# Building the first rows of a decoder trunk another way: where the modulation sums, the norm and the rows are made

## The chip, the cores and the metric

The kernel runs on one core of one Trainium2 chip. The metric is the device time of one execution in microseconds (us). A core has five engines that work beside each other, each through its own list of instructions in the order in which they stand: TensorE (PE, with its weight loads PEld), VectorE (DVE), ScalarE (ACT), GpSimd (POOL) and SyncE (SP), which here issues every DMA transfer. An engine that waits for another holds up all that stands behind in its own list.

## The reference

Two layers run over 256 tokens of width 2048: a retention mixer and then a gated short convolution, each followed by a SwiGLU feed-forward network. Ahead of every sub-layer the tokens are normalised and modulated by a conditioning vector `c`:

```python
def rms_norm(x, gain=None):
    xf = x.astype(jnp.float32)
    y = xf * lax.rsqrt(jnp.mean(xf * xf, axis=-1, keepdims=True) + EPS)
    if gain is not None:
        y = y * gain.astype(jnp.float32)
    return y

c_act = jax.nn.silu(c)
for i in range(DEPTH):                                            # DEPTH = 2
    mod = (c_act @ w_mod[i] + b_mod[i])[:, None, :]
    sh1, sc1, g1, sh2, sc2, g2 = jnp.split(mod, 6, axis=-1)       # each 2048 wide
    h = (rms_norm(x, norm1_g[i]) * (1.0 + sc1) + sh1).astype(x.dtype)
    # m = i % 4: 0 is retention, 1 is the short convolution
    x = (x + g1 * y).astype(x.dtype)                              # y is the mixer's output for h
    h = (rms_norm(x, norm2_g[i]) * (1.0 + sc2) + sh2).astype(x.dtype)
    x = (x + g2 * swiglu(h, ffn_w_in[i], ffn_w_out[i])).astype(x.dtype)
return rms_norm(x, final_g).astype(x.dtype)
```

The change touches the first `h` alone, which the retention mixer multiplies by its input weights (queries, keys, values and gates).

## The kernel before, in words

All activations lie with channels on the 128 partitions and the 256 tokens along them, so `x` and `h` are 16 rows of 128 channels each (KT = 16). "Row" always means such a block of 128 channels below.

Every float32 product is made of three products of parts kept in the type `fp32r`: high times high, high times low, low times high. So a weight block from memory is cut into a high part (`hi`, a CAST on ACT, L295) and a low part (`lo`, a subtraction on DVE, L296). The weights lie in memory in the order of their use, in pieces of 128 x 2048 (1 MiB each, one transfer). `prepare()` cuts half a piece, 128 x 1024, at a time; half a piece serves eight blocks of 128 x 128, which is 24 products on PE. Four `hi` and four `lo` buffers are used in turn, and three for the pieces as they come from memory. A row `h[k]` is cut into high and low in the same way.

A modulation value is a sum over 2048 products. One transfer brings 128 rows of `w_mod` (1 MiB), one DVE instruction over 128 x 2048 multiplies them by `cb`, the activated `c` on all partitions, and sums (L238), and one or two small POOL instructions add bias and gain (L243, L245, L248). Each row of the first `h` needs two of these: its scale (SC1) and its shift (SH1).

The first layer begins in two stages, and they are where the change is:

- **First stage** (`RET_FIRST`, lines 588 to 594). 16 column blocks (the first two heads' queries, keys and gates) are multiplied by the first `FIRST_KS = 11` rows, as soon as each row is made. Each row brings 48 products, one piece of weights (two halves) and two modulation sums: three transfers of 1 MiB. The order on DVE and ACT is as the code is written there (`tc.manual_schedule`).
- **Second stage** (lines 595 to 603). Three more heads' columns are multiplied by the same 11 rows, two column blocks at a time, in 12 groups. The sine and cosine tables (`angles`) and the five rows that are left are made beside it. Here a scheduler puts DVE's and ACT's instructions into an order; PE's and the transfers' order is as written. `held()` copies each finished group from PSUM with ACT (L569).

After that come the heads themselves (which add the products with the rows that were left out), the output projection, and the rest of the trunk. The order of PE's instructions is as written everywhere. Modulation sums of later sub-layers are spread over the whole run by a plan of PE's progress (`paced`).

The start is: `c` comes as one row, is spread to all partitions by products with ones (L199) and activated out of PSUM (L200); squares of the 16 rows of `x` on ACT (L387), added up on DVE (L388); sums over partitions on PE (L396), root by POOL's power (L407), spread on PE (L414), copied by ACT (L577). Then for each row k, in `row(k)` and `scale`:

- `scaled` (L424, DVE): u = x times scale column times root,
- `shifted` (L431, ACT): high part of u + shift, and (L432, DVE) its low part,
- the sum for SC1 of row k + 1 between these two, and the sum for SH1 of row k + 1 after half of row k's products.

Of the kernel before, what the change touches and what calls it, by code (L numbers as in the profile page):

```python
# [33 lines left out]
FIRST_KS = 11  # L34
EARLY_HEADS = 5
START_RAWS = 3
# [19 lines left out]
class Group:  # L56
    """Output columns of a matrix that are worked out together, in the order of their rows."""
# [60 lines left out]
def in_use_order():  # L118
    """Each group of the weights, with its matrix and the matrix's index, in the order of use."""
# [23 lines left out]
def laid_out(arrays):  # L143
    """The weights in the order of their use, as blocks of 128 rows and CHUNK columns."""
    total = sum(len(g.cols) * g.width * len(g.ks) for _, _, g in in_use_order())
    out = np.empty((total // CHUNK, P, CHUNK), np.float32)
    at = 0
    for key, i, g in in_use_order():
        for k in g.ks:
            for c in g.cols:  # L150
                o = at % CHUNK
                out[at // CHUNK, :, o : o + g.width] = arrays[key][i, k * P : (k + 1) * P, c : c + g.width]
                at += g.width
    assert at == total and total % CHUNK == 0
    return out
# [16 lines left out]
def trunk(ctx: ExitStack, tc: tile.TileContext, x_in, c_in, pos_in, w_mod, cols_in, tab_in, w_all, out):  # L172
# [8 lines left out]
    def name(s):  # L181
        serial[0] += 1
        return f"{s}_{serial[0]}"
# [10 lines left out]
    with tc.tile_pool(name="crow", bufs=1) as cp:  # L194
        row = cp.tile([1, D], F32, tag="row", name="row")
        nc.sync.dma_start(row, c_in)
        for i in range(0, D, 2 * S):
            pt = ps.tile([P, 2, S], F32, tag="bank", name=name("bank")).rearrange("p a b -> p (a b)")
            nc.tensor.matmul(pt, ones[0:1, :], row[:, i : i + 2 * S], start=True, stop=True)  # L199
            nc.scalar.activation(cb[:, i : i + 2 * S], pt, AF.Silu)  # L200
    x = []
    for i in range(0, KT, 4):
        t = const.tile([P, 4, S], F32, tag=f"x{i}", name=f"x{i}")
        nc.sync.dma_start(t, x_in[:, i : i + 4, :])
        x += [t[:, j, :] for j in range(4)]
    n_cols = cols_in.shape[1]
    cols = const.tile([P, n_cols], F32, tag="cols", name="cols")
    nc.sync.dma_start(cols, cols_in)
# [13 lines left out]
    nc.sync.dma_start(tab, tab_in[:, : 1 + P])  # L222
# [9 lines left out]
    def modulation(layer, which, j, pool=wpool, bufs=RAW_BUFS):  # L232
        t = layer * 6 * KT + which * KT + j
        raw = pool.tile([P, CHUNK], F32, tag="raw", name=name("raw"), bufs=bufs)
        nc.sync.dma_start(raw, w_mod[t])
        total = tmp("msum", (P, 1), bufs=4)
# [23 lines left out]
    def paced(n):  # L260
        """Counts n more products of 128 x 128 weights, and works out the modulations due by now."""
# [18 lines left out]
    ready, taken_cols, raws = [], [0], []  # L280

    def prepare():
# [5 lines left out]
        if i == 0:  # L288
            raw = wpool.tile([P, CHUNK], F32, tag="raw", name=name("raw"), bufs=RAW_BUFS)
            nc.sync.dma_start(raw, w_all[n * HALF // CHUNK])  # L290
            raws[:] = [raw]
# [9 lines left out]
    def take(group, k, col):  # L301
        """The next weights' high and low parts."""
# [18 lines left out]
    def ticked(n):  # L321
        """Between products, the next step of what runs beside them."""
# [5 lines left out]
    def product(g, act, base=0, before=None, banks=None, last=True):  # L328
        """Banks [columns, (high product, the rest), tokens], one for each of the group's columns."""
# [18 lines left out]
    def packed(g, act, base=0, before=None, between=None, banks=None):  # L348
        """Banks [columns, two of the group's columns, tokens]."""
# [25 lines left out]
    def split(dst, src, at=slice(0, S)):  # L375
        """dst [128, (high, low), tokens] of src."""
# [14 lines left out]
    def norm_sums(accs):  # L391
        """The sums over partitions, a token to a partition."""
# [9 lines left out]
    def norm_roots(pt, n):  # L402
        """1 / sqrt(mean + eps)."""
# [6 lines left out]
    def norm_spread(r):  # L410
        """The roots on all partitions, in PSUM."""
# [32 lines left out]
    def scaled_only(layer, norm, j):  # L444
        """h[j] without the norm and the shift."""
# [54 lines left out]
    def output(groups, act, which, last, after=None):  # L500
        """x += gate * product; if last, tiles whose sums are those of the new x's squares."""
# [24 lines left out]
    with ExitStack() as inner:  # L526
# [45 lines left out]
        with tc.tile_pool(name="start", bufs=1) as sp:  # L572
            acc = None
            for j in range(KT):
                acc = squares(acc, x[j])
            rb = tmp("rb", pool=sp, bufs=1)
            nc.scalar.copy(rb, rstd([acc], D))  # L577

            def scale(which, k):
                if k < KT:  # L580
                    modulation(0, which, k, sp, START_RAWS)

            def row(k):
                u = scaled(k, rb, 0, 0)
                scale(SC1, k + 1)
                shifted(h[k], u, k, 0, 0)

            with tc.manual_schedule(engines={mybir.EngineType.DVE, mybir.EngineType.Activation}):
                scale(SC1, 0)
                scale(SH1, 0)  # L590
                banks = [bank() for _ in range(8)]
                pts = packed(RET_FIRST, h, before=row, between=lambda k: scale(SH1, k + 1), banks=banks)
# [77 lines left out]
        def mixed(head, both, v, sg):  # L670
            """The rest of a head, in steps."""
# [32 lines left out]
        def pair(head, i):  # L704
            """Two columns' sums [columns, two, tokens]."""
# [143 lines left out]
```

## Time and profile before

| What | Value |
|---|---|
| Time, median of 3 runs | 2667.12 us (2664.53 to 2668.72) |
| Span of the profiled execution | 2660.6 us (first to last instruction) |
| PE busy | 2621.9 us, 99% of the span |
| DVE busy | 2017.8 us, 76% |
| ACT busy | 1248.4 us, 47% |
| POOL busy | 214.0 us, 8% |
| Transfers | 687.69 MB, mean 258 GB/s |
| Granted TensorE clock, mean | 0.998 |

The page gives the span and no other time of its execution; the span lies 6.5 us under the median of the timed runs. How to read it: busy times are sums of instructions' durations on an engine, and a PE product of 256 columns is shown with 0.28 us though a new one starts every 0.12 us, since products overlap in the array. So 99% says that PE almost always has something in flight. The first 40th of the span (66 us) is the exception: the row of busy tenths for PE begins with a 6.

### The profile page before, as it was taken

Reading aid. Unit: us, or ns where it says so; the run is one execution under the profiler, and the core shown is the slowest. Engines: PE = TensorE matmul, PEld = TensorE weight load, DVE = VectorE, ACT = ScalarE, POOL = GpSimd, SP = SyncE. Lnnn points to the kernel's source line nnn. Section 1 sums busy time; section 2 is a strip of 40 time slices with the busy share of each in tenths; the row PEclk is TensorE's granted clock in tenths of the full one; section 3 lists DMA queues with packets and bytes.
Section 4 is the critical chain, followed back from the end, with each engine's and each line's share of the span. In section 5 each row is a group of like instructions: output and inputs, shape, how many; then the busy total and the mean of one; then the engine's idle time right before and its main releaser. Section 6 shows DMA issues by size and latency. Waiting matters only on the chain.

```text
span 2660.6 us, 40134 instructions
## 1 busy us (share of the span) xinstructions
PE 2621.9 (99%) x16044; PEld 2335.6 (88%) x16044; DVE 2017.8 (76%) x2655; ACT 1248.4 (47%) x1782; POOL 214.0 (8%) x278
## 2 busy tenths in 40 slices
PE   6999999999999999999999999999999999999998
PEld 5898988999989888888888898888998888888887
DVE  8968988887698877777777889878887665555554
ACT  3444543444456444334444454444554443444443
POOL 4310000011000010100000001100000000000000
PEclk9999999999999999999999999999999999999999
DMA  9976667777677877777777768776777765555553
GB/s 374 400 265 242 251 217 296 267 270 263 250 267 261 312 281 267 298 271 284 285 268 282 268 219 321 287 282 256 268 269 256 264 220 190 185 185 189 189 190 127
DMA packets 96957, 687.69 MB, mean 258 GB/s; under 512 B 10753, under 2 KB 12545, under 8 KB 13825
## 3 DMA queue, kind: packets, MB, share of 16 engines
q1 hardware_dynamic: 96770, 685.13, 69.3%
q8 instruction: 125, 2.05, 0.3%
q14 instruction: 62, 0.51, 0.1%
HBM read 682.99 MB, written 2.10 MB: 257 GB/s over the span
## 4 chain that ended last, share of the span: by engine, by line
PE 76%; issue 19%; DVE 3%; DMA 0%; POOL 0%; ACT 0%; DVEq 0%; ACTq 0%; POOLq 0%
PE bank L338 35%; PE bank L341 18%; PE bank L363 4%; PE bank L361 4%; PE bank L362 4%; PE bank L634 2%; PE bank L635 2%; PE bank L636 2%; PE bank L477 1%; PE bank L476 1%; PE bank L478 1%; DVE raw L238 1%; DVE lo L296 1%; PE bank L680 0%; DMA raw<-w_mod 0%
## 5 line engine op out<-in xcount | busy, mean ns | idle before, releaser
L296 DVE TENSOR_TENSOR lo<-raw,hi 128x1024 fp32r<-128x1024 f32 x912 | 1113.5, 1223 | 561.1 <-ACT hi L295 559.2
L295 ACT CAST hi<-raw 128x1024 fp32r<-128x1024 f32 x912 | 953.9, 1050 | 1087.3 <-PE bank L338 638.5
L338 PE MATMUL bank<-h,hi 128*128 128x512 f32 x3296 | 1155.2, 395 | 0.0
L341 PE MATMUL bank<-h,lo 128*128 128x256 f32 x3296 | 925.5, 281 | 0.0
L338 PEld LDWEIGHTS bank<-h,hi 128*128 128x128 f32 x3296 | 622.7, 189 | 144.9
L338 PE MATMUL bank<-mid,hi 128*128 128x512 f32 x2100 | 731.1, 395 | 0.1
L341 PEld LDWEIGHTS bank<-h,lo 128*128 128x128 f32 x3296 | 623.3, 189 | 0.0
L341 PE MATMUL bank<-mid,lo 128*128 128x256 f32 x2100 | 583.8, 278 | 0.0
L338 PEld LDWEIGHTS bank<-mid,hi 128*128 128x128 f32 x2100 | 394.1, 188 | 92.2 <-DVE mid L378 0.4
L238 DVE SCALAR_TENSOR_TENSOR raw<-raw,cb 128x2048 f32<-128x2048 f32 x192 | 438.5, 2284 | 5.0 <-DMA raw<-w_mod 4.8
L341 PEld LDWEIGHTS bank<-mid,lo 128*128 128x128 f32 x2100 | 395.0, 188 | 0.0
L363 PE MATMUL bank<-h,lo 128*128 128x256 f32 x1024 | 292.4, 286 | 10.0 <-DVE lo L296 10.0
L361 PE MATMUL bank<-h,hi 128*128 128x256 f32 x1024 | 290.6, 284 | 2.8 <-ACT hi L295 2.8
L362 PE MATMUL bank<-h,hi 128*128 128x256 f32 x1024 | 290.3, 284 | 0.6 <-DVE h L432 0.5
L363 PEld LDWEIGHTS bank<-h,lo 128*128 128x128 f32 x1024 | 193.8, 189 | 14.4 <-DVE lo L296 14.4
L361 PEld LDWEIGHTS bank<-h,hi 128*128 128x128 f32 x1024 | 195.7, 191 | 3.5 <-ACT hi L295 3.3
L362 PEld LDWEIGHTS bank<-h,hi 128*128 128x128 f32 x1024 | 193.9, 189 | 2.3 <-DVE h L432 2.3
L243 POOL TENSOR_SCALAR mcol<-msum,cols 128x1 f32<-128x1 f32 x64 | 63.6, 994 | 549.6 <-DVE raw L238 549.6
L634 PE MATMUL bank<-hi,h 128*128 128x512 f32 x256 | 101.4, 396 | 0.0
L635 PE MATMUL bank<-lo,h 128*128 128x512 f32 x256 | 101.0, 395 | 0.0
L636 PE MATMUL bank<-hi,h 128*128 128x512 f32 x256 | 101.0, 394 | 0.0
L370 ACT COPY low<-bank 128x256 f32<-128x256 f32 x254 | 90.7, 364 | 11.7 <-PE bank L341 9.0
(122 smaller groups left out, 1811.6 us busy)
## 6 DMA issues: line engine op xcount, KB each, us to landing
raw<-w_all SPq DMA_DIRECT2D x456, 1024.0 KB, 4.9
raw<-w_mod SPq DMA_DIRECT2D x192, 1024.0 KB, 5.0
x<-x_in SPq DMA_DIRECT2D x4, 512.0 KB, 5.7
out<-out SPq DMA_DIRECT2D x5, 256.0 KB, 2.9
decay<-tab_in SPq DMA_DIRECT2D x8, 128.0 KB, 3.0
out<-out SPq DMA_DIRECT2D x3, 128.0 KB, 2.3
out<-out SPq DMA_DIRECT2D x1, 384.0 KB, 2.7
cols<-cols_in SPq DMA_DIRECT2D x1, 160.0 KB, 7.2
```

The costliest lines, as they stand in the source:

```text
L238: nc.vector.scalar_tensor_tensor(raw, raw, 1.0, cb, op0=ALU.mult, op1=ALU.mult, accum_out=total)
L295: nc.scalar.copy(hi, raw)
L296: nc.vector.tensor_tensor(lo, raw, hi.bitcast(F32), op=ALU.subtract)
L338: nc.tensor.matmul(pt, hi, h, start=fresh and k == g.ks[0], stop=False, skip_group_check=True)
L341: nc.tensor.matmul(pt[:, 1, :], lo, h[:, 0, :], start=False, stop=last and k == g.ks[-1], skip_group_check=True)
L361: nc.tensor.matmul(pt, hi, h[:, 0, :], start=first, stop=False, skip_group_check=True)
L362: nc.tensor.matmul(pt, hi, h[:, 1, :], start=False, stop=False, skip_group_check=True)
L363: nc.tensor.matmul(pt, lo, h[:, 0, :], start=False, stop=last, skip_group_check=True)
L370: nc.scalar.copy(low[:, at], pt[:, 1, at])
L634: nc.tensor.matmul(o, ht[:, 0, :], hi, start=k == 0, stop=False)
L635: nc.tensor.matmul(o, ht[:, 0, :], lo, start=False, stop=False)
L636: nc.tensor.matmul(o, ht[:, 1, :], hi, start=False, stop=k == KT - 1)
```

## The change

- **c**: one transfer now writes `c` to all 128 partitions (`c_in.to_broadcast([P, D])`, 128 rows of 8 KiB), and one ACT instruction over 128 x 2048 activates it in place. The products with ones are gone.
- **Norm**: ACT squares `x` two rows at a time (8 instructions of 128 x 512), and PE sums all of them into one place, four products of one column for each; DVE's 15 additions are gone.
- **Normalised rows**: `norm_two` multiplies two rows of `x` by the root at once on DVE (128 x 512).
- **Columns**: for the first 16 rows, ACT makes scale and shift columns (`column`, 128 x 1) from the sums; POOL makes none of them any more. `gain_1` is prepared once.
- **Rows**: ACT makes each row twice from the normalised one with scale and shift, in full float32 and as the high part; DVE subtracts (128 x 256, two tensors).
- **Order**: both sums of row k + 1 stand together, after half of row k's products; then `norm_two` in every second row; then the second half's `lo`. Transfers are issued two rows ahead, with `START_RAWS = 4` buffers for `w_mod` instead of 3, and weights' pieces are fetched apart from being cut.
- **Span**: `FIRST_KS = 10`. So the first stage has 480 products instead of 528 and the second 720 instead of 792; six rows instead of five are made beside the second stage, and the 48 products of row 10 in the first stage go to the heads.
- In the second stage, the sums of `both_reduced` no longer carry the low priority `MOD_PRIO`.

The same change, cut to its core (removed comments and docstrings are left out):

```diff
-FIRST_KS = 11
+FIRST_KS = 10
-START_RAWS = 3
+START_RAWS = 4
...
-            acc = None
-            for j in range(KT):
-                acc = squares(acc, x[j])
-            rb = tmp("rb", pool=sp, bufs=1)
-            nc.scalar.copy(rb, rstd([acc], D))
-
-            def scale(which, k):
-                if k < KT:
-                    modulation(0, which, k, sp, START_RAWS)
-
-            def row(k):
-                u = scaled(k, rb, 0, 0)
-                scale(SC1, k + 1)
-                shifted(h[k], u, k, 0, 0)
+            def reduced(which, k):
+                if k < KT:
+                    raw = raws_of.pop((which, k))
+                    total = totals[which, k] = tmp("msum", (P, 1), bufs=4)
+                    nc.vector.scalar_tensor_tensor(raw, raw, 1.0, cb, op0=ALU.mult, op1=ALU.mult, accum_out=total)
+
+            def column(which, k):
...
+                nc.scalar.activation(dst, totals.pop((which, k)), AF.Identity, bias=bias, scale=scale)
+                return dst
...
+            def row(k, between=None):
+
+                a, b = column(SC1, k), column(SH1, k)
+                t = normed_x[k // 2][:, k % 2, :]
+                full = tmp("u", bufs=3)
+                nc.scalar.activation(full, t, AF.Identity, bias=b, scale=a)
+                nc.scalar.activation(h[k][:, 0, :], t, AF.Identity, bias=b, scale=a)
+                if between:
+                    between()
+                nc.vector.tensor_tensor(
+                    h[k][:, 1, :], full, h[k][:, 0, :].bitcast(F32), op=ALU.subtract
+                )
+
+            def both_reduced(k):
+                reduced(SC1, k + 1)
+                reduced(SH1, k + 1)
+                if k % 2 == 0 and k + 2 < KT:
+                    norm_two(k // 2 + 1)
+                ahead_of(k + 2)
...
+                    row(k, prepare)
+
+                pts = packed(RET_FIRST, h, before=before, between=both_reduced, banks=banks)
...
                 for k in late[i * len(late) // n : (i + 1) * len(late) // n]:
                     row(k)
-                    scale(SH1, k + 1)
+                    both_reduced(k)
```

How the instructions stand now is shown at three places. Names: `raw` with `msum` is a modulation sum (L238, now L581), `lo<-raw,hi` a low half of a weight piece, `hi<-raw` a high half, `two` two normalised rows, `u` a row in full, `a` and `s` the columns of scale and shift.

First, DVE in the first stage, one row before (row 4):

```order
L424 SCALAR_TENSOR_TENSOR u_503<-x_92,a_104,rb_173 128x256
L238 SCALAR_TENSOR_TENSOR raw_505,msum_507<-raw_505,cb 128x2048
L432 SCALAR_TENSOR_TENSOR h<-u_503,s_108,h 128x256
L296 TENSOR_TENSOR lo_517<-raw_514,hi_516 128x1024
L238 SCALAR_TENSOR_TENSOR raw_544,msum_546<-raw_544,cb 128x2048
L296 TENSOR_TENSOR lo_550<-raw_514,hi_549 128x1024
```

and one row of the change with `norm_two` (row 2), up to the first instructions of the next:

```order
L294 TENSOR_TENSOR lo_350<-raw_242,hi_349 128x1024
L609 TENSOR_TENSOR h<-u_346,h 128x256
L581 SCALAR_TENSOR_TENSOR raw_310,msum_378<-raw_310,cb 128x2048
L581 SCALAR_TENSOR_TENSOR raw_312,msum_380<-raw_312,cb 128x2048
L598 TENSOR_TENSOR two_382<-x_73,rb_183 128x512
L294 TENSOR_TENSOR lo_391<-raw_242,hi_390 128x1024
L294 TENSOR_TENSOR lo_424<-raw_314,hi_423 128x1024
L609 TENSOR_TENSOR h<-u_420,h 128x256
```

The two sums no longer lie on both sides of a half's `lo`; they follow each other, and between the second of them and the next row's first `lo` stand only `two` (in every second row) and one `lo`.

Second, ACT in the first stage, from one row's last cast to the next row's casts; before:

```order
L431 ACTIVATE h<-u_281,s_108 128x256
L295 CAST hi_294<-raw_292 128x1024
L295 CAST hi_327<-raw_292 128x1024
L431 ACTIVATE h<-u_355,s_108 128x256
L295 CAST hi_368<-raw_366 128x1024
L295 CAST hi_401<-raw_366 128x1024
```

and in the change:

```order
L293 CAST hi_316<-raw_121 128x1024
L590 ACTIVATE a_80<-msum_306,gain_123,cols 128x1
L590 ACTIVATE s_84<-msum_308,cols 128x1
L605 ACTIVATE u_346<-two_236,s_84,a_80 128x256
L606 ACTIVATE h<-two_236,s_84,a_80 128x256
L293 CAST hi_349<-raw_242 128x1024
L293 CAST hi_390<-raw_242 128x1024
```

A row's first cast now stands behind four ACT instructions of that row, the second of which reads the second sum (`msum_308`).

Third, DVE where the second stage begins; before, from the first stage's last `lo` (`lo_994`) to the second stage's first (`lo_1078`):

```order
L296 TENSOR_TENSOR lo_994<-raw_958,hi_993 128x1024
L533 CAST acc_1040<-u_1038 128x256
L534 TENSOR_SCALAR acc_1040<-acc_1040,tab 128x256
L549 TENSOR_SCALAR u_1045<-acc_1040 128x256
L549 TENSOR_SCALAR u_1059<-acc_1040 128x256
L550 TENSOR_SCALAR u_1045<-u_1045 128x256
L550 TENSOR_SCALAR u_1059<-u_1059 128x256
L551 TENSOR_SCALAR u_1045<-u_1045 128x256
L551 TENSOR_SCALAR u_1059<-u_1059 128x256
L555 SCALAR_TENSOR_TENSOR sum_1049<-u_1045,acc_1040 128x256
L296 TENSOR_TENSOR lo_1078<-raw_1075,hi_1077 128x1024
```

and in the change, from `lo_897`:

```order
L294 TENSOR_TENSOR lo_897<-raw_752,hi_896 128x1024
L581 SCALAR_TENSOR_TENSOR raw_892,msum_1062<-raw_892,cb 128x2048
L581 SCALAR_TENSOR_TENSOR raw_894,msum_1064<-raw_894,cb 128x2048
L531 CAST acc_943<-u_941 128x256
L532 TENSOR_SCALAR acc_943<-acc_943,tab 128x256
```

then the same six steps of `angles` as before (`u_948`, `u_962`), and behind them, up to the second stage's first `lo` (`lo_981`):

```order
L549 TENSOR_SCALAR u_962<-u_962 128x256
L553 SCALAR_TENSOR_TENSOR sum_952<-u_948,acc_943 128x256
L609 TENSOR_TENSOR h<-u_1058,h 128x256
L553 SCALAR_TENSOR_TENSOR sum_954<-u_948,sum_952 128x256
L294 TENSOR_TENSOR lo_981<-raw_978,hi_980 128x1024
```

Two sums of 128 x 2048 (row 11's), row 10's subtraction and one more step of `angles` have come between the two `lo`.

More of the change, by code (lines that the diff above doesn't have):

```diff
@@ L193, in trunk @@
     cb = const.tile([P, D], F32, tag="cb", name="cb")
[L194 to L205, printed above, removed]
+    x4 = [const.tile([P, 4, S], F32, tag=f"x{i}", name=f"x{i}") for i in range(0, KT, 4)]
+    x = [t[:, j, :] for t in x4 for j in range(4)]
     n_cols = cols_in.shape[1]
     cols = const.tile([P, n_cols], F32, tag="cols", name="cols")
-    nc.sync.dma_start(cols, cols_in)
     at = [0]
@@ L279, in trunk, with fetch @@
     n_halves = w_all.shape[0] * CHUNK // HALF
-    ready, taken_cols, raws = [], [0], []
+    ready, taken_cols, raws, fetched, n_fetched = [], [0], [], [], [0]
+    def fetch():
+        raw = wpool.tile([P, CHUNK], F32, tag="raw", name=name("raw"), bufs=RAW_BUFS)
+        nc.sync.dma_start(raw, w_all[n_fetched[0]])
+        n_fetched[0] += 1
+        fetched.append(raw)
     def prepare():
@@ L288, in prepare @@
         if i == 0:
-            raw = wpool.tile([P, CHUNK], F32, tag="raw", name=name("raw"), bufs=RAW_BUFS)
-            nc.sync.dma_start(raw, w_all[n * HALF // CHUNK])
-            raws[:] = [raw]
+            if not fetched:
+                fetch()
+            raws[:] = [fetched.pop(0)]
         raw = raws[0][:, i : i + HALF]
@@ L591, in trunk, with before @@
                 banks = [bank() for _ in range(8)]
-                pts = packed(RET_FIRST, h, before=row, between=lambda k: scale(SH1, k + 1), banks=banks)
+                def before(k):
+                    row(k, prepare)
+                pts = packed(RET_FIRST, h, before=before, between=both_reduced, banks=banks)
                 for i, pt in enumerate(pts):
```

60 lines of the change are left out of this document (55 added, 5 removed).

## The prediction

> I forecast 2679 us, some 12 us slower.
>
> **What bounds the kernel now.** I read the busy times by stretches first, to find where PE is not full, since it is busy for 99% of the span.
>
> ```profile
> 80.00:100.00 20.00, 17.40 (x131) 16.01 (x132) 19.75 (x21) 5.52 (x7) 10.62 (x8) 1.00 1.01 420
> 100.00:120.00 20.00, 18.79 (x151) 17.98 (x150) 19.93 (x35) 14.01 (x20) 4.70 (x3) 1.00 0.91 359
> 120.00:140.00 20.00, 20.00 (x170) 20.00 (x170) 16.50 (x19) 9.07 (x12) 4.17 (x6) 1.00 0.85 340
> 300.00:1000.00 700.00, 699.49 (x4432) 631.00 (x4432) 577.48 (x799) 340.18 (x507) 55.12 (x86) 1.00 0.72 269
> 2000.00:2600.00 600.00, 600.00 (x3438) 524.54 (x3438) 361.06 (x440) 274.63 (x379) 6.26 (x10) 1.00 0.57 207
> ```
>
> The columns are the stretch, its length, then PE, PEld, DVE, ACT and POOL, the clock, the transfers' share and GB/s. From 120 us on PE is full. So the time is decided by how early PE gets through the first rows; what a faster DVE or POOL does later is worth nothing. In the first stage DVE is full (19.75 of 20), and the transfers are too (420 GB/s). One row on DVE, from the timeline:
>
> ```profile
> 45.63 0.48 DVE L424 SCALAR_TENSOR_TENSOR u<-x,a,rb 128x256 f32<-128x256 f32 x1
> 46.02 2.29 DVE L238 SCALAR_TENSOR_TENSOR raw<-raw,cb 128x2048 f32<-128x2048 f32 x1
> ...
> 48.23 0.49 DVE L432 SCALAR_TENSOR_TENSOR h<-u,s,h 128x256 fp32r<-128x256 f32 x1
> 48.63 1.22 DVE L296 TENSOR_TENSOR lo<-raw,hi 128x1024 fp32r<-128x1024 f32 x1
> 49.77 2.29 DVE L238 SCALAR_TENSOR_TENSOR raw<-raw,cb 128x2048 f32<-128x2048 f32 x1
> ...
> 51.98 1.23 DVE L296 TENSOR_TENSOR lo<-raw,hi 128x1024 fp32r<-128x1024 f32 x1
> 53.12 0.48 DVE L424 SCALAR_TENSOR_TENSOR u<-x,a,rb 128x256 f32<-128x256 f32 x1
> ```
>
> Start to start: u 0.39, a sum 2.21 (twice), h 0.40, a `lo` 1.14 (twice): a row every 7.49 us without a gap. DVE never waits for ACT, because each sum's column is needed half a row later. Three transfers of 1.049 MB at 420 GB/s take 7.49 us as well. The stage's end:
>
> ```profile
> 104.82 1.21 DVE L296 TENSOR_TENSOR lo<-raw,hi 128x1024 fp32r<-128x1024 f32 x1
> 105.96 0.28 DVE L533 CAST acc<-u 128x256 f32<-128x256 int32 x1
> 106.32 0.28 PE L361 MATMUL bank<-h,hi 128*128 128x256 f32 x1
> 108.22 1.22 DVE L296 TENSOR_TENSOR lo<-raw,hi 128x1024 fp32r<-128x1024 f32 x1
> 108.84 0.28 PE L361 MATMUL bank<-h,hi 128*128 128x256 f32 x1
> 109.49 0.39 PE L363 MATMUL bank<-h,lo 128*128 128x256 f32 x1 [0.26 <-DVE lo L296]
> ```
>
> PE starts the second stage's first low product at 109.49, 4.67 after the last `lo` of the first stage began, with a wait of 0.26. Between 106.32 and 108.84 lie 21 products: 0.120 each. This 109.49 is the mark against which I count; from there on PE's work is fixed, plus the 48 products that the change puts off, 48 x 0.120 = 5.76. The change breaks even if its own mark lies at 103.73.
>
> **The change part by part.**
>
> *Start.* The transfers ahead of the last part of x are now: c 1.05 MB, columns 0.16, x 2.10, one `w_mod` 1.05, together 4.36 MB. Two stretches, an issue on SP's queue with its time to landing, and the norm's chain:
>
> ```profile
> 0.00:5.00 5.00, 2.37 (x3) 1.16 (x4) 0.17 (x2) 1.28 (x1) 0.19 (x4) 1.00 0.50 150
> 5.00:15.00 10.00, 4.79 (x6) 1.33 (x4) 5.38 (x13) 8.77 (x20) 0.00 (x0) 1.00 1.03 416
> 6.62 0.33 SPq L290 DMA_DIRECT2D raw<-w_all  x1
> raw<-w_all SPq DMA_DIRECT2D x1, 1024.0 KB, 13.6
> 18.28 1.01 PE L396 MATMUL bank<-ones,acc 128*128 128x1 f32 x4 [8.48 <-DVE acc L388]
> 20.65 0.72 POOL L407 TENSOR_TENSOR rs<-rs,half 128x2 f32<-128x2 f32 x1
> 21.42 1.22 PE L414 MATMUL bank<-tab,rs 128*128 128x128 f32 x4 [2.13 <-POOL rs L407]
> 22.68 0.37 ACT L577 COPY rb<-bank 128x256 f32<-128x256 f32 x1 [7.09 <-PE bank L414]
> 26.17 1.22 DVE L296 TENSOR_TENSOR lo<-raw,hi 128x1024 fp32r<-128x1024 f32 x1
> ```
>
> 0.75 MB by 5 us, then 0.416 MB/us: 4.36 MB pass by 13.7. The first weight piece (6.5 MB with all ahead of it, so 19.0) landed at 6.62 + 13.6 = 20.2, 1.2 later; so x is there at 14.9. Then two squares of 128 x 512 (1.1, by the groups below), sums 1.0, root's input 0.2, power 0.8, spread 1.2, copy 0.4: 19.6. `norm_two` 0.8, u and h 1.0, cast 1.05 and small waits: the first `lo` starts at 22.6, where it was 26.17. SH1's sum of row 0 fits between. No row shows c read 128 times: the low bound is that it costs the queue nothing (-2.5), the high one that it takes twice its bytes' time (+2.5). I take its bytes, as for the other pieces.
>
> *The rows.* The prices:
>
> ```profile
> L448 ACT ACTIVATE h<-x,a 128x256 fp32r<-128x256 f32 x48 | 23.8, 495 | 0.0
> L755 ACT ACTIVATE silu<-sum 128x256 f32<-128x256 f32 x88 | 36.6, 416 | 85.8 <-DVE sum L372 85.7
> L491 ACT COPY end<-bank 128x1 f32<-128x1 f32 x18 | 2.2, 146 | 0.0
> L295 ACT CAST hi<-raw 128x1024 fp32r<-128x1024 f32 x912 | 953.9, 1050 | 1087.3 <-PE bank L338 638.5 <-DMA raw<-w_all 112.5 <-PE bank L362 100.5
> L200 ACT ACTIVATE cb<-bank 128x512 f32<-128x512 f32 x4 | 2.4, 595 | 0.0
> L711 DVE TENSOR_TENSOR qs<-ahead,bank 128x512 f32<-128x512 f32 x20 | 13.6, 681 | 1.7 <-PE bank L363 1.6
> L378 DVE TENSOR_TENSOR mid<-m,mid 128x256 fp32r<-128x256 f32 x88 | 36.8, 418 | 0.5 <-ACT mid L377 0.5
> L569 ACT COPY ahead<-bank 128x512 f32<-128x512 f32 x20 | 11.5, 584 | 6.9 <-PE bank L363 6.5
> 9.92 5.22 DVE L388 TENSOR_TENSOR acc<-acc,sq 128x256 f32<-128x256 f32 x10 [0.37 <-ACT sq L387]
> 53.69 0.51 ACT L431 ACTIVATE h<-u,s 128x256 fp32r<-128x256 f32 x1 [5.10 <-DVE u L424]
> ```
>
> DVE's own work falls: two sums 4.42, two `lo` 2.28, the subtraction 0.42 - 0.08 = 0.34, half of a `norm_two` 0.30: 7.34 instead of 7.49 (0.08 is the overlap of a `lo`, 1.22 against 1.14). But the order makes a ring of it. The next row's first `lo` needs its `hi`, which stands on ACT behind the SH1 column, u and h, and that column needs the second sum. While ACT does this, DVE has one `lo` (1.14), and in every second row 0.60 more. ACT's part: the wake-up 0.09 (u at 53.12 lasts 0.48, h starts at 53.69), the column 0.25, the wait of u for it 0.10 (as in the chain of ten additions, 522 ns each for an operation of about 420), u and h 0.48 each, the cast 1.05, the wake-up of DVE 0.03: 2.48. For u and h I add 0.08, the difference between one column operand (495) and none (416), to 0.50, and take off 0.10 of overlap. The bounds: 2.14 (column as L491, no wait, u and h at 0.41) and 2.83 (column 0.50, wait 0.20). So a row takes `lo` 1.14 + subtraction 0.34 + sums 4.42 + the second one's end 0.08 + 2.48 = 8.46 us, bounds 8.12 and 8.81. That is longer than the transfers' 7.49, so these fall behind no more.
>
> POOL's columns lay beside half a row of DVE's work and are gone: 0. Loading two rows ahead gives 0 too: DVE, not a late transfer, ended a row before, and the ring does now. In the start it keeps the queue full, which is in the bytes above.
>
> *The end of the stage.* Rows 0 to 9: the last row's first `lo` starts at 22.6 + 9 x 8.46 = 98.7, its second 5.90 later (1.14 + 0.34 + 4.42), at 104.6. Then DVE does two sums more (4.42), the nine steps of `angles` (105.96 to 108.22: 2.26), a subtraction and one step more (0.68), before the second stage's first `lo`. That one ends at 104.6 + 1.14 + 4.42 + 2.26 + 0.68 + 1.22 = 114.3, the mark at 114.4. ACT's cast for it stands behind s of row 11, h and u, and is done earlier, some 8.1 after 104.6 against 8.5. PE has 2.8 us of work in the meantime, so it idles more than 4 us, where it idled 0.26.
>
> *Clock.* A pause of that length may cost more than itself:
>
> ```profile
> 27.82 0.41 PE L361 MATMUL bank<-h,hi 128*128 128x256 f32 x1
> 30.81 0.42 PE L363 MATMUL bank<-h,lo 128*128 128x256 f32 x1
> ```
>
> 14 products in 2.99 us, 0.214 each, in the first 3.2 us of PE's dense work; later 0.120. If PE begins the second stage so, some 16 products lose 0.094 each: 1.5. No row shows a long pause after dense work, so I take 0.75 between 0 and 1.5. The Trainium skill (TensorE: Matmul & The Clock Gate, "Part 1: The HAM clock gate") has the clock halved after an idle window of about 3.4 us and given back after as long a busy one; by that the term is 1.5, and the pauses of about 2.5 us inside each row cost nothing.
>
> *Second stage.* In the third group ACT's list has the copy of the finished group (0.48 start to start) ahead of a cast whose half is wanted 0.5 x 2.86 = 1.43 us later. Copy, cast 1.05, `lo` 1.22 and PE's own end 0.28 make 3.0: up to 1.5 of waiting, less where PE is late anyway; I take 0.75. Otherwise DVE has 12 groups x 7.2 = 86 us for 30 `lo` at 1.14 and four rows' sums at 4.42, 52 us, and a few us of small ones.
>
> *Sum.* 114.4 + 5.76 - 109.49 = +10.7, clock 0.75, copy 0.75: +12.2 on a span of 2660.6. With the 6.5 us between span and median, 2679.3; I say 2679.
>
> **The rivals.**
>
> *The ring is hidden* (not slower). If the ACT part is at most what DVE does beside it (1.14, or 1.74 in every second row), rows come at the transfers' 7.49. Then the mark is 22.6 + 9 x 7.49 + 15.7 = 105.7 and the change +2.0: 2669, no change that can be told. For it speaks that ACT is idle for most of a row (5.52 of 20); against it that the four instructions and the cast stand in line behind the sum. It decides at an ACT part of 1.4 us. To get faster by over 0.2%, the start would have to be at its low bound and the boundary's 5.1 gone as well: 2661.5.
>
> *The clock falls in every row.* PE is through a row's first half 4.5 after the first `lo` begins (1.6 until the subtraction's end, 24 products) and has the second `lo` at 7.1: it pauses some 2.5 us. If all 48 products then take 0.214, a row takes 10.3 us, 1.8 more: +16.2, 2695. Against it: the first row's slow stretch ended after 3.2 us and none came back, and PE works 5.8 of each 8.5 us.
>
> *The transfers set the pace.* If they sink to the 359 GB/s of the stretch from 100 to 120 us, a row's 3.146 MB take 8.76 us, which adds 9 x 0.30 = 2.7: 2682. The 420 GB/s of the stretch before speaks against it, and a ring that needs only 372. The Trainium skill (DMA: Bandwidth & Descriptors, "Specifications") gives a core about 358 GB/s from memory, by which this rival would hold; the 420 measured here differ.
>
> **How the numbers follow.** Chances: the forecast 0.75, the hidden ring 0.12, the clock 0.04, the transfers 0.04, faster than all these 0.05. The forecast's own range adds the bounds: below -2.5 (start), -3.1 (rows), -0.75, -0.75: 2672; above +2.5, +3.2, +0.75, +0.75: 2686. To hold eight in ten, with half of the hidden ring's cases, I take 2668 to 2687. What can be told from no change is 0.2%, 5.3 us: faster 0.05, same 0.13 (the hidden ring and a little of the forecast's low end), slower 0.82.
>
> **What would show it.** In the profile after: the first `lo` near 22.6; DVE with gaps of about 1 us before each first `lo`, released by ACT's cast; first `lo` 8.1 to 8.8 us apart; the first low product of the second stage near 114 with PE idle over 4 us ahead of it, and perhaps slow products behind. A row every 7.3 to 7.6 us, or a mark below 104, would prove me wrong.

## The result and the profile after

| | before | changed |
|---|---|---|
| Time, median | 2667.92 us (2664.53 to 2669.06, 4 runs) | 2686.88 us (2684.46 to 2687.19, 4 runs) |
| Span of the profiled execution | 2660.6 us | 2684.9 us |
| First `lo` | 26.17 | 30.17 |
| A row of the first stage | 7.49 | 8.41 |
| First low product of the second stage (the mark) | 109.49 | 121.52 |

The changed kernel takes 1.0072 times as long (95% interval 1.0058 to 1.0086): 19.0 us more, where 12 were forecast. The two profiled executions lie further apart than the medians, by 24.3 us, because that of before was one of the quicker ones: in every profiled run whose time is on record the time lies about 2 us above the span, so the one of before took some 2662.5 us, where the median is 2667.92.

The start, from the timeline of the changed kernel. The columns are start, duration, engine, line, operation, and in brackets the idle time ahead of it and what ended that.

```profile
8.85 13.81 PE L651 MATMUL bank<-ones,sq 128*128 128x1 f32 x64 [8.85 <-ACT sq L648]
14.58 1.15 ACT L648 ACTIVATE sq<-x 128x512 f32<-128x512 f32 x2 [0.20 <-DMA x<-x_in]
22.70 0.16 DVE L403 TENSOR_SCALAR rs<-bank 128x2 f32<-128x2 f32 x1 [8.36 <-PE bank L651]
22.77 2.28 DVE L581 SCALAR_TENSOR_TENSOR raw<-raw,cb 128x2048 f32<-128x2048 f32 x1
22.94 2.67 POOL L405 TENSOR_TENSOR rs<-rs,half 128x2 f32<-128x2 f32 x1 [22.51 <-DVE rs L403]
25.66 1.22 PE L412 MATMUL bank<-tab,rs 128*128 128x128 f32 x4 [3.00 <-POOL rs L405]
30.17 1.22 DVE L294 TENSOR_TENSOR lo<-raw,hi 128x1024 fp32r<-128x1024 f32 x1 [2.15 <-ACT hi L293]
```

The squares are done at 14.58 + 1.15 = 15.73, but the sums over partitions only at 22.66. The 32 products in the code are 64 instructions, each with weights of its own, which start 0.216 us apart and queue up on PE: the squares take 7.6 us, their sums 13.8. Then the root takes 2.67 us on POOL, where it took 0.72.

One row of the first stage, on DVE and ACT:

```profile
46.99 1.23 DVE L294 TENSOR_TENSOR lo<-raw,hi 128x1024 fp32r<-128x1024 f32 x1 [1.29 <-ACT hi L293]
50.67 2.29 DVE L581 SCALAR_TENSOR_TENSOR raw<-raw,cb 128x2048 f32<-128x2048 f32 x1
53.01 0.29 ACT L590 ACTIVATE s<-msum,cols 128x1 f32<-128x1 f32 x1 [1.82 <-DVE raw L581]
53.33 0.60 ACT L605 ACTIVATE u<-two,s,a 128x256 f32<-128x256 f32 x1
53.49 1.22 DVE L294 TENSOR_TENSOR lo<-raw,hi 128x1024 fp32r<-128x1024 f32 x1
53.84 0.59 ACT L606 ACTIVATE h<-two,s,a 128x256 fp32r<-128x256 f32 x1
54.33 1.98 ACT L293 CAST hi<-raw 128x1024 fp32r<-128x1024 f32 x2
55.39 1.23 DVE L294 TENSOR_TENSOR lo<-raw,hi 128x1024 fp32r<-128x1024 f32 x1 [0.68 <-ACT hi L293]
```

Here is the ring: the second sum ends, ACT makes s, u, h and the cast in line, and DVE waits 0.68 us (1.29 in the rows without a `norm_two`; in two rows a second `norm_two` fills the gap) for the half it needs first. Row to row it is 55.39 - 46.99 = 8.40.

The end of the stage:

```profile
111.76 1.22 DVE L294 TENSOR_TENSOR lo<-raw,hi 128x1024 fp32r<-128x1024 f32 x1
112.89 2.28 DVE L581 SCALAR_TENSOR_TENSOR raw<-raw,cb 128x2048 f32<-128x2048 f32 x1
115.10 2.28 DVE L581 SCALAR_TENSOR_TENSOR raw<-raw,cb 128x2048 f32<-128x2048 f32 x1
119.84 0.41 PE L359 MATMUL bank<-h,hi 128*128 128x256 f32 x1 [3.92 <-ACT hi L293]
120.25 1.22 DVE L294 TENSOR_TENSOR lo<-raw,hi 128x1024 fp32r<-128x1024 f32 x1
121.52 0.58 PE L361 MATMUL bank<-h,lo 128*128 128x256 f32 x1 [1.05 <-DVE lo L294]
146.91 0.38 PE L359 MATMUL bank<-h,hi 128*128 128x256 f32 x1 [0.21 <-ACT hi L293]
148.17 0.39 PE L361 MATMUL bank<-h,lo 128*128 128x256 f32 x1 [0.76 <-DVE lo L294]
```

Between the last `lo` of the first stage (111.76) and the first of the second (120.25) stand two more sums and the steps of `angles`. PE idles 3.92 and 1.05 us. Its clock, from the windows view (stretch, length, PE, PEld, DVE, ACT, POOL with their counts, clock, transfers' share, GB/s):

```profile
40.00:60.00 20.00, 15.20 (x113) 14.73 (x112) 18.02 (x19) 7.71 (x13) 0.00 (x0) 0.91 0.97 349
89.00:93.00 4.00, 4.00 (x24) 4.00 (x23) 3.96 (x5) 1.11 (x3) 0.00 (x0) 0.57 0.93 377
120.00:124.00 4.00, 2.94 (x13) 2.65 (x14) 4.00 (x8) 3.28 (x5) 0.00 (x0) 0.51 0.70 258
124.00:128.00 4.00, 4.00 (x25) 4.00 (x24) 4.00 (x8) 0.26 (x1) 0.00 (x0) 0.64 0.91 348
128.00:132.00 4.00, 4.00 (x36) 4.00 (x35) 4.00 (x4) 0.89 (x3) 0.00 (x0) 1.00 1.01 424
```

The last two rows have 25 and 36 products in 4 us: behind the pause PE goes at half pace, until about 126.8. The 23 products from 121.89 on that started 0.213 apart in place of 0.120 lost 2.1 us. DVE is no longer full in the rows (18.02 of 20).

### The profile page after: what moved, and what is told of

Read it like the earlier page. It is cut to its first block, busy times and chain, and to the rows that moved or that the text cites. A ratio compares the mean times of both kernels' runs of the same rounds, so it can differ in the third digit from the quotient of the medians.

```text
span 2684.9 us, 40179 instructions
## 1 busy us (share of the span) xinstructions
PE 2633.0 (98%) x16096; PEld 2352.8 (88%) x16096; DVE 2010.4 (75%) x2633; ACT 1262.7 (47%) x1818; POOL 158.9 (6%) x230
## 4 chain that ended last, share of the span: by engine, by line
PE 72%; issue 20%; DVE 5%; ACT 1%; POOL 1%; DMA 0%; DVEq 0%; ACTq 0%; POOLq 0%
PE bank L336 34%; PE bank L339 17%; PE bank L361 4%; PE bank L360 4%; PE bank L359 4%; PE bank L710 2%; PE bank L708 2%; PE bank L709 2%; DVE raw L581 2%; PE bank L475 1%; PE bank L474 1%; PE bank L476 1%; DVE lo L294 1%; ACT hi L293 1%; POOL rs L405 1%
## 5 line engine op out<-in xcount | busy, mean ns | idle before, releaser
L230 DVE SCALAR_TENSOR_TENSOR raw<-raw,cb 128x2048 f32<-128x2048 f32 x160 | 365.3, 2283 | 7.6 <-DMA raw<-w_mod 7.4
L359 PE MATMUL bank<-h,hi 128*128 128x256 f32 x1024 | 293.8, 287 | 7.4 <-ACT hi L293 7.4
L360 PE MATMUL bank<-h,hi 128*128 128x256 f32 x1024 | 293.5, 287 | 1.0 <-DVE h L609 1.0
L240 POOL TENSOR_TENSOR g<-msum,cols 128x1 f32<-128x1 f32 x64 | 37.5, 585 | 879.3 <-DVE raw L230 879.3
```

Of the source, the lines that this page charges most:

```text
L230: nc.vector.scalar_tensor_tensor(raw, raw, 1.0, cb, op0=ALU.mult, op1=ALU.mult, accum_out=total)
L359: nc.tensor.matmul(pt, hi, h[:, 0, :], start=first, stop=False, skip_group_check=True)
L360: nc.tensor.matmul(pt, hi, h[:, 1, :], start=False, stop=False, skip_group_check=True)
```

## The experiments

My theory T names three causes: the late start, the ring in the rows, and the end of the stage. The rival R lays start and rows on the transfers, since c comes with 1 MB more and loads stand two rows ahead, and since only 349 GB/s were moved between 40 and 60 us, where the kernel before moved 392 in that stretch and 420 from 80 to 100. Besides the times I use one place late in the same work: POOL's first root of the heads (L405), at 268.95 us in the changed kernel. Single executions differ in x's landing at the start by up to 0.8 us, which goes into that place too.

**The norm's sums.** In the loop over squares:

```diff
-reduced(SC1, 0)
 ...
-    for n in range(4): nc.tensor.matmul(pt[...], sq[...], ones[:, 0:1], ...)
+    if i == 0: first_sq = sq
+    else: nc.vector.tensor_tensor(first_sq, first_sq, sq, op=ALU.add)
+    if i == 3: reduced(SC1, 0)
+for n in range(4): nc.tensor.matmul(pt[...], first_sq[...], ones[:, 0:1], ...)
```

> The changed kernel, with the eight squares of c added up by seven VectorE additions of 128x512 and only the total summed by TensorE (4 products in place of 32); nothing is left out. Theory T (the late start comes from TensorE: 64 passes of 0.216 us queue up and end at 22.66): the last sum ends near 18.3, the first `lo` comes near 25.8 in place of 30.17, and the time falls by about 4.4 us. Theory R (the late start and the slow rows come from the transfers, c's extra 1 MB and the deeper queue of loads): the first `lo` stays above 28 and the time within 1 us of the changed kernel.

Timeline of this run:

```profile
17.69 1.87 PE L657 MATMUL bank<-ones,sq 128*128 128x1 f32 x8 [17.69 <-DVE sq L652]
19.84 2.67 POOL L405 TENSOR_TENSOR rs<-rs,half 128x2 f32<-128x2 f32 x1 [19.41 <-DVE rs L403]
27.07 1.23 DVE L294 TENSOR_TENSOR lo<-raw,hi 128x1024 fp32r<-128x1024 f32 x1 [2.15 <-ACT hi L293]
```

Eight instructions take 1.87 us and the first `lo` comes 3.1 us earlier, not 4.4: the last four of DVE's additions now queue behind its first modulation sum and end only at 17.64. 2681.61 us, 1.0058 of before (1.0041 to 1.0075); the root of the heads lies 3.5 us earlier. R had the first `lo` above 28, and it came at 27.07: the sums on PE were a cause. What held the root at 2.67 is the next question.

**POOL's power.** I had put the 2.67 us down to POOL's first real operation. So an unused power was added at the very start:

```diff
+woken = const.tile([P, 2], F32, ...)
+nc.gpsimd.tensor_tensor(woken, ones[:, 0:2], half, op=ALU.pow)
```

> The changed kernel, with one more power on POOL at its very start, on two columns of ones, which nobody reads. T (POOL's first operation is dear, 2.67 us, wherever it stands): the root of c's sums takes about 0.72 us, as in the kernel before, and the first `lo` comes 1.95 us earlier, near 28.2. R: the root stays at about 2.7 us because its operands or the transfers hold it, and the first `lo` stays near 30.2.

```profile
1.09 0.69 POOL L215 TENSOR_TENSOR woken<-ones,half 128x2 f32<-128x2 f32 x1 [0.66 <-DVE half L213]
22.85 2.28 DVE L583 SCALAR_TENSOR_TENSOR raw<-raw,cb 128x2048 f32<-128x2048 f32 x1
23.01 2.67 POOL L407 TENSOR_TENSOR rs<-rs,half 128x2 f32<-128x2 f32 x1 [21.23 <-DVE rs L405]
```

2685.09 us in one run. My reason falls: the first power took 0.69 us and the second still 2.67. But the rows show another one. A DVE sum starts 0.16 ahead of the power and ends at 25.13, the power 0.55 later. So the next run moved that sum, out of the power's way and into DVE's 8.36 us of waiting for PE:

```diff
-r = norm_roots(pt, D)
 reduced(SH1, 0)
+r = norm_roots(pt, D)
```

> The changed kernel, with VectorE's second sum of row 0 (2.28 us) put ahead of the root of c's and x's norm in place of beside it, into VectorE's pause while TensorE sums the squares; nothing else. T2 (formed after the extra power at the start, which took 0.69 us while the later one still took 2.67: POOL's power is held up by the VectorE sum that runs beside it): the power takes about 0.7 us and the first `lo` comes at 28.2 in place of 30.17. T (the power is dear when POOL has long been idle): it stays at 2.67 us and the first `lo` at 30.2.

```profile
23.05 0.69 POOL L405 TENSOR_TENSOR rs<-rs,half 128x2 f32<-128x2 f32 x1 [22.62 <-DVE rs L403]
28.30 1.23 DVE L294 TENSOR_TENSOR lo<-raw,hi 128x1024 fp32r<-128x1024 f32 x1 [2.15 <-ACT hi L293]
```

The power takes 0.69 us and the first `lo` comes at 28.30, as T2 had it (2682.74 us in one run; the root of the heads 1.7 earlier). The power waits for the sum beside it. The Trainium skill (SBUF — State Buffer, "Who interferes with whom") says that a VectorE instruction with two inputs in SBUF contends with a GpSimd instruction that reads SBUF, that the port pair which they share is an exclusive lock, and that the order of issue decides who blocks. The sum has two such inputs and starts first, and the trace agrees, with 2.67 against 0.69.

**The ring.** ScalarE's cast goes ahead of the columns in `row`:

```diff
 def row(k, between=None):
+    if between: between()
     a, b = column(SC1, k), column(SH1, k)
 ...
-    if between: between()
     nc.vector.tensor_tensor(h[k][:, 1, :], full, ...)
```

> The changed kernel, with ScalarE's cast of the next block put ahead of the columns, u and h of the row in place of behind them, so that VectorE's low part never waits for them. T (the ring of cast, low part, second block and columns sets 8.41 us a row): the first low parts come 7.3 to 7.5 us apart, VectorE's waits of 0.68 and 1.29 us in each row go, and the time falls by about 8 us (nine rows of 0.9). R (the transfers set the row): the rows stay at 8 us or more and the time within 1 us.

```profile
49.94 2.36 DVE L294 TENSOR_TENSOR lo<-raw,hi 128x1024 fp32r<-128x1024 f32 x2
56.96 1.23 DVE L294 TENSOR_TENSOR lo<-raw,hi 128x1024 fp32r<-128x1024 f32 x1
102.16 1.22 DVE L294 TENSOR_TENSOR lo<-raw,hi 128x1024 fp32r<-128x1024 f32 x1
```

and a stretch of its rows, in the columns of the windows view:

```profile
40.00:60.00 20.00, 16.12 (x132) 15.52 (x131) 20.00 (x23) 10.16 (x17) 0.00 (x0) 1.00 0.99 397
```

DVE has no gap left (20.00 of 20); a row takes 7.0 to 7.64 us, the larger with a `norm_two`, and 7.63 in every row from 64.60 to 95.14, where further `norm_two` stand in the rows that had none. The first `lo` is also 1.87 earlier (28.30), since its cast no longer waits for row 0's u and h. The last second `lo` starts at 102.16 in place of 111.76. 2674.99 us, 1.0030 of before (1.0015 to 1.0045); the root of the heads 10.1 us earlier. With the same loads in the same order the rows came 0.8 us closer, so the transfers did not set them; they moved 397 GB/s in the stretch that had 349. ACT's casts do wait for four pieces between 28 and 108 us now, 6.1 us in all, but DVE, which sets the row, does not. R falls for the rows.

**The end of the stage, by order.** First three halves of the second stage ahead of the late sums, then two halves, between the copies of the finished banks:

```diff
-    if k < FIRST_KS: fetch()
+    if k < FIRST_KS + 2: fetch()
 ...
 pts = packed(RET_FIRST, h, ...)
+for _ in range(3): prepare()
 for i, pt in enumerate(pts):
     held(i // 4, i % 4, pt)
+    # second try: none above, FIRST_KS + 1, and here: if i == 3: two times prepare()
```

> The changed kernel, with the first two rows of the second stage loaded, cast and given their low parts ahead of the last first-stage row's sums and angles in place of behind them. T (the pause of TensorE at the end of the first stage, 3.92 and 1.05 us, and its products at half pace for some 7 us behind it come from the sums standing ahead of the low parts): the pause and the half pace go, and the time falls by 6.5 to 7 us. R (TensorE waits for the transfers of the second stage there): pause and time stay within 1 us.

> The changed kernel, with only two halves of the second stage's weights cast and given their low parts ahead of row 11's sums, and these behind the first four and ahead of the last four copies of the finished banks on ScalarE (in the first try three casts stood ahead of all copies, the third waited, and TensorE waited 7.05 us for the banks). T (the pause at the end of the first stage comes from casts and low parts standing behind row 11's sums and columns): TensorE goes on into the second stage at about 116.5 with no pause over 1 us, pauses 1 to 2 us some 5.7 us later, keeps its clock, and the time falls by 4 to 6 us. R (the pause is set by the transfers or the banks): pause and time stay within 1.5 us.

The first try, then the second, from their timelines:

```profile
121.41 0.29 ACT L590 ACTIVATE s<-msum,cols 128x1 f32<-128x1 f32 x1 [1.83 <-DVE raw L581]
122.24 1.03 ACT L293 CAST hi<-raw 128x1024 fp32r<-128x1024 f32 x1
123.18 3.98 ACT L567 COPY ahead<-bank 128x512 f32<-128x512 f32 x8
123.80 0.58 PE L359 MATMUL bank<-h,hi 128*128 128x256 f32 x1 [7.05 <-ACT ahead L567]
```

```profile
125.55 0.39 PE L361 MATMUL bank<-h,lo 128*128 128x256 f32 x1 [1.18 <-DVE lo L294]
132.47 0.39 PE L359 MATMUL bank<-h,hi 128*128 128x256 f32 x1 [1.21 <-ACT hi L293]
135.00 0.39 PE L361 MATMUL bank<-h,lo 128*128 128x256 f32 x1 [2.03 <-DVE lo L294]
```

2685.32 us (1.0074, 1.0059 to 1.0089) and 2687.69 us (1.0081, 1.0067 to 1.0094): nothing gained in either, where T had expected 4 to 7 us. In the first try the late sums held PE up by another way: a column that waited for one of them stood on ACT ahead of the third cast and of the eight copies, and PE waited 7.05 us for the banks. In the second the long pause is gone, and 4.4 us of shorter ones stand where there were 5.0. So T is wrong on this point: these orders only move the pause. R's transfers do not fit either, as no engine waits for one from 108 to 137 us in either run. What stays is the amount: in the changed kernel DVE is busy for all but 0.07 of the 24 us from 108 to 132.

**The end of the stage, by amount.** The second stage multiplies rows 0 to 9 alone, so nothing in it needs the sums of rows 10 and 11. They are loaded and done later:

```diff
 def both_reduced(k):
-    reduced(SC1, k + 1); reduced(SH1, k + 1)
+    if k + 1 < FIRST_KS: reduced(SC1, k + 1); reduced(SH1, k + 1)
 def ahead_of(k):
-    loaded(SC1, k); loaded(SH1, k)
-    if k < FIRST_KS: fetch()
+    if k < FIRST_KS: loaded(SC1, k); loaded(SH1, k)
+    if k < FIRST_KS + 2: fetch()
 ...                                     # the later rows, in the second stage
+    loaded(SC1, k); loaded(SH1, k); reduced(SC1, k); reduced(SH1, k)
     row(k)
```

> The changed kernel, in which the sums of rows 10 and 11 (two of 2.21 us each row) are neither loaded nor done in the first stage and at its end; each of the six later rows is loaded and summed in the second stage, where it was turned into h before. Everything is still computed. T3 (formed after the two tries at the order, where the pause of TensorE only moved: the pause comes from the amount of VectorE's work at the boundary, 8.84 us of sums that nothing in the second stage needs): the last second `lo` comes 4.4 us earlier, at 107.3, the second stage's first ones right behind it, TensorE's pause of 3.92 and 1.05 us and the 2.1 us at half pace go: 10 to 12 us less than the changed kernel. R (those sums only move and hold TensorE up later in the second stage): less than 4 us.

Timeline and windows of this run:

```profile
104.91 0.39 PE L361 MATMUL bank<-h,lo 128*128 128x256 f32 x1 [2.95 <-DVE lo L294]
```

```profile
120.00:140.00 20.00, 20.00 (x172) 20.00 (x171) 17.95 (x25) 13.01 (x20) 0.00 (x0) 1.00 0.94 377
```

2676.41 us, 1.0038 of before (1.0025 to 1.0051), 10.5 us below the changed kernel (9 by the two ratios), with the root of the heads 10.4 earlier. The row of 104.91 is the last in the stage and behind it at which PE waits at all; from 120 to 140 it is full at full clock. T3 holds: the pause, the slow products behind it and the waits at 146.91 and 148.17 are all gone. The two weight pieces that are fetched sooner do not explain it, since the first try at the order fetched them too.

**All causes together**, with the halves ahead (the second try), with the deferred sums, and this with a first span of eight rows:

> The changed kernel with all four causes taken away together: squares added up by VectorE, row 0's second sum ahead of the root, the cast ahead of the columns, and the second stage's first two halves ahead of row 11's sums. T: first `lo` at 23.5, rows 7.64 us apart, the last second `lo` at about 97.5, TensorE without a pause over 2 us at the end of the stage: 17 to 19 us less than the changed kernel, so within 3 us of the kernel before. R (the causes overlap and hide one another): less than 14 us in all.

> The kernel with three causes taken away (squares added up by VectorE and row 0's second sum ahead of the root; the cast ahead of the columns), and with the deferred sums of the run before this one in place of the second stage's halves ahead of the sums. T3: first `lo` at 23.1, last second `lo` at 92.5, no pause over 2 us behind it: 8 to 10 us less than with the halves ahead, so 3 to 5 us faster than the kernel before. R: no more than 3 us less than with the halves ahead, so slower than the kernel before.

> The same with a first span of eight rows in place of ten. T3 (a row of the first stage costs 7.64 us there and 48 products, 5.76 us, when it is put off): 3.8 us faster than with ten rows. R (eight later rows, two sums each, are more than VectorE can do beside the 12 groups of the second stage, which shrink to 8 rows each): slower than with ten rows.

| | time, us | of before (95%) | first `lo` | root of the heads |
|---|---|---|---|---|
| changed kernel | 2686.88 | 1.0072 (1.0058 to 1.0086) | 30.17 | 268.95 |
| start, ring, halves ahead | 2670.76 | 1.0020 (1.0011 to 1.0029) | 23.08 | 253.42 |
| start, ring, deferred sums | 2661.09 | 0.9984 (0.9976 to 0.9993) | 23.00 | 244.19 |
| the same, span of eight | 2683.99 | 1.0065 (1.0052 to 1.0078) | 23.41 | not the same work |

By the root of the heads the single runs add up: 3.5 + 1.7 + 10.1 = 15.3, and 15.5 measured with the halves ahead; with 10.4 for the deferred sums 25.7, and 24.8 measured. The causes hardly hide one another. T had expected 17 to 19 us less with the halves ahead, within 3 us of the kernel before; it was 16.1 less and 5.0 above it, as those halves bring nothing. T3's 8 to 10 us less than this came true with 9.7. The version with deferred sums is the fastest of all, 0.16% below the kernel before: the interval leaves out 1, though the difference is smaller than the 0.2% that I set as telling. With a span of eight, the 3.8 us that T3 expected turned into 23 lost. From the timeline of that run:

```profile
122.87 0.29 ACT L590 ACTIVATE s<-msum,cols 128x1 f32<-128x1 f32 x1 [0.90 <-DVE raw L581]
124.20 3.87 ACT L293 CAST hi<-raw 128x1024 fp32r<-128x1024 f32 x4
125.28 0.58 PE L359 MATMUL bank<-h,hi 128*128 128x256 f32 x1 [3.93 <-ACT hi L293]
145.50 0.59 ACT L567 COPY ahead<-bank 128x512 f32<-128x512 f32 x1 [3.13 <-PE bank L361]
148.39 0.58 PE L359 MATMUL bank<-h,hi 128*128 128x256 f32 x1 [2.93 <-ACT hi L293]
172.28 0.58 PE L359 MATMUL bank<-h,hi 128*128 128x256 f32 x1 [3.32 <-ACT hi L293]
```

PE pauses again and again in the second stage, 3 to 4 us at a time. R has the sign, but not its reason: DVE is not out of time there (busy for 15.4, 13.7 and 14.9 of 20 us from 120 to 180). ACT's cast of 124.20 stands behind a row's column, u and h, and the column waits for the row's sum: the ring again, now in the second stage. At the other two pauses the sums are long done; there column, u, h and cast all stand behind the copy of a finished group (145.50 and 169.00), which itself waits for PE. Both are read from the trace. Whether another order would make the span of eight pay was not tried.

**The span alone.** The kernel before with `FIRST_KS = 10`:

> The kernel before, with a first span of ten rows in place of eleven and nothing else of the change. T (the span by itself is nearly free: the mark comes 7.49 us earlier and 48 products of 0.120 us come behind it): 1.7 us faster than the kernel before, between -3 and +1. R (a shorter first span costs by itself, by a later pause at the boundary or in the second stage): slower than the kernel before by over 3 us.

2665.52 us, 0.9997 of before (0.9988 to 1.0005). Its PE waits give back part of what the earlier boundary brings:

```profile
101.66 0.39 PE L363 MATMUL bank<-h,lo 128*128 128x256 f32 x1 [0.28 <-DVE lo L296]
114.39 0.39 PE L363 MATMUL bank<-h,lo 128*128 128x256 f32 x1 [1.06 <-DVE lo L296]
126.75 0.39 PE L363 MATMUL bank<-h,lo 128*128 128x256 f32 x1 [0.71 <-DVE lo L296]
```

The mark is 7.83 us earlier, 5.76 come back as products and 1.77 as waits: 0.3 in all. So 0 or a little, as T had it within its bounds; the span as such is no part of the loss.

## Why the prediction was right and where it was wrong

The direction, the ring in the rows and the size of the boundary were right; the start was wrong. The forecast time was 8 us too low, and from span to span the kernel became 24.3 us longer where 12.2 were forecast. That 2686.88 lies inside the range, by 0.1, is luck, as the sum below shows.

- *The rows*: right. 8.41 us measured, 8.46 forecast, with ACT's part 2.43 (52.96 to 55.39) for 2.48, and the run with the cast first shows that the ring is the cause.
- *The end of the stage*: right in size. From the last second `lo` to the mark 9.76 us, 9.78 forecast. My reading that the order makes the pause was wrong in the first theory; the amount of sums does, and the prediction had counted just that (4.42 for row 10's sums ahead of the last second `lo`, 4.42 for row 11's behind it).
- *Start*: the step that failed. The forecast had the first `lo` at 22.6, and it came at 30.17: 7.6 too early. Two of its terms are to blame. "Sums 1.0" took the price of the row before, four instructions for one total, where the change makes 64; with 0.216 each they end 6.9 us behind the last square, 5.9 too late. "Power 0.8" was a row without a DVE sum beside it; with one it is 2.67, and root and input together cost 2.0 more than forecast. The landing of x was right (squares done at 15.73 against 16.0, though 6.5 MB pass at 18.8 by the prediction's own figures, not at 19.0), and so was the rest from the spread to the first `lo` (4.5 us against 4.6).
- *Clock*: half pace did follow, and its size was 2.1 us, not 0.75; the upper bound of 1.5 was too low. The slow stretch lasted 7 us (119.84 to 126.8), not 3.2. The Trainium skill's rule of an idle window (TensorE: Matmul & The Clock Gate, "Part 1: The HAM clock gate") gave the sign; the 1.5 us worked out by it were too little.
- *Second stage*: the copy ahead of a cast cost its upper bound, 1.5 (the four steps from the product at 146.42 to that at 148.40, with the waits at 146.91 and 148.17, take 1.98 us in place of 0.48), not 0.75.
- *Sum*: the mark lies 12.0 later, 5.76 for the products put off, 2.1 and 1.5: 21.4 of the 24.3 us between the spans. The other 2.9 stay open. A part of them may be scatter between executions: two stretches with PE full (404.55 to 537.01 and 537.01 to 609.90 by POOL's roots) take 131.09 and 72.36 to 72.38 in most runs of the changed kernel and its variants, and 132.46 and 72.89 here, 1.9 more; but the first try at the order and the run with the deferred sums took 132.47 for the first of them too, and what decides is not known. Of the 12.1 us by which the forecast of the span was short, the late start makes 7.1 at the mark, the clock 1.4, the copy 0.75 and this rest 2.9. Against it stands the 6.5 us from span to median, which the forecast took over from before and which was 2.0 here. That error of 4.5 us the other way is what keeps the time inside the range.
- *The rivals*: the ring is not hidden. The clock falls in every second row from 54 us on (0.91 in the mean), but costs no time, as PE still waits 0.3 us for DVE at the end of such a row. The transfers do not set the pace.

## What to carry to other kernels

A price from a row holds for its count and its neighbours: ask how many instructions the new code makes of one line, and what runs beside them. Where an in-order engine makes a value for another and then must serve it with the next one, put first what the other engine needs first; here that was worth 0.8 us a row. And before work at a boundary is put into another order, see whether it is needed there at all: two orders gained nothing, leaving 8.84 us of sums for later gained 10.

## What the runs showed of the hardware that I had not expected

- Products with one moving column and new weights of 128 x 128 float32 for each take 0.216 us an instruction at a granted clock of 1.00, two instructions for one product in the code: 13.8 us for 32, more than adding the same squares on DVE (0.77 us for 128 x 512) and summing once (1.87).
- A POOL operation on 128 x 2 goes from 0.69 to 2.67 us if a 2.28 us DVE sum starts just ahead of it, and ends 0.55 us behind it. The 1.51 and 2.09 us of POOL's columns before, with DVE sums beside them, may be the same; that was not tried.
- Slow products do not follow every pause, and not at once. In the changed kernel, 3.20 us between two products (85.20 to 88.40) were followed by seven at full pace and then 3.4 us at half (89.34 to 92.75; the clock of 0.57 in the windows above). The prediction had taken such pauses as free by the idle window of about 3.4 us that the Trainium skill gives (TensorE: Matmul & The Clock Gate, "Part 1: The HAM clock gate"); in time they were. But that length does not fit as the least pause: in the second try at the boundary, 2.1 us between two products (78.13 to 80.25) were enough, while in the run with the cast first 1.9 to 2.0 us in each row from 64 us on were not. The windows of these two, in that order:

```profile
80.00:100.00 20.00, 16.37 (x113) 15.97 (x114) 17.34 (x20) 9.71 (x16) 0.00 (x0) 0.86 0.99 364
```

```profile
80.00:100.00 20.00, 15.51 (x126) 15.11 (x127) 20.00 (x22) 9.30 (x15) 0.00 (x0) 1.00 0.97 396
```

What decides between them, the length or where the pause lies in time, stays open.
